# The operand of the gated mixer's short convolutions is kept in PSUM instead of SBUF

## The chip, the cores and the metric

The kernel runs on one core of a Trainium2 chip. The metric is the device time of one execution in microseconds; three runs of the kernel before and, later, of the kernel after are compared by their medians.

## The reference

Two model blocks run one after the other on 256 tokens of width 1024, all in float32. The first block has three kinds of attention, a gated MLP with a width-3 convolution and a per-layer embedding gate. The second has two layers, each a mixer, a cross attention to a memory and a squared-ReLU MLP. The mixer of its second layer (`c_mixer`) is a gated delta rule, and only the start of it matters here:

```python
def short_conv(x, w):
    K = w.shape[0]                               # 4 taps
    T = x.shape[1]                               # 256 tokens
    xp = jnp.pad(x, ((0, 0), (K - 1, 0), (0, 0)))
    return sum(xp[:, j:j + T] * w[j] for j in range(K))

qkv, gate, b, a = _split(h @ w_in, C_SIZES)      # 3072 channels of q, k, v
qkv = jax.nn.silu(short_conv(qkv, conv_w))       # per channel, along the tokens
q, k, v = _split(qkv, (GDN_QK, GDN_QK, GDN_VW))
q = l2norm(...); k = l2norm(...)                 # 8 heads of 128
```

`h` is the RMS-normed input. The kernel multiplies the un-normed operand by the weights and scales the product by the row factor `R` (one value per token) afterwards.

## The kernel before

Everything lies transposed: channels on the 128 partitions, the 256 tokens along the free axis. float32 products are made of three fp32r products: each operand is cut into a high and a low half, and hi*hi, hi*lo and lo*hi are summed in PSUM.

**Weights.** They come in 188 chunks through a ring of three. `fetch` (L438) loads a chunk in two halves of 128x1024. ScalarE (ACT) casts each half to `hi`, and then `lo` = raw - hi is made on VectorE (DVE) or on GpSimd (POOL); a hand-made list (`W["pool"]`) says how many of a chunk's two halves go to POOL.

**Products.** `gemm_ab` (L472) issues 48 matmuls of 128x256 into one PSUM tile, `pg`: a bank of 128x512 float32, that is 128 channels x 2 groups x 256 tokens. The pool of `pg` has two banks. So product n+2 goes into the bank of product n, and its first matmul waits until everything that reads product n there is done. Between its matmuls `pump` lets other work of the mixer issue its small matmuls at times that a planner's table gives; on TensorE (PE) the order is then fixed as written.

**Order on the other engines.** The framework orders the instructions of each engine by a timeline that it works out when the program is built, and adds every semaphore. An engine takes its instructions in that order. Two instructions on different engines that touch the same PSUM tile are kept in the order in which the program states them.

**The convolutions.** `conv` (L1441) runs twelve times. I number them: conv 1 to 4 are q and k of heads 0 to 3, conv 5 and 6 are values, conv 7 to 10 are q and k of heads 4 to 7, conv 11 and 12 are values. Each takes the product `ps`, scales it by `R` into an SBUF tile `u` (L1447, DVE, 128x512), and then, for each of its two groups, makes one output `cc[:, i]` of four taps: the first tap is a scaled copy on ACT, the other three are multiply-adds on DVE (`stt`, L377), each on `u` shifted by one, two or three tokens. `cc` lies in a part of the tile `Vm`, so in the trace a tap is `Vm<-u,cols` on ACT and `Vm<-u,cols,Vm` on DVE. `u` is one of four buffers that other temporaries share: the squares of q and k, the SiLU of v, three tiles of the gates and the output gates' SiLU.

**What follows a convolution.** For q and k (`qk_then`, L1464) ACT makes the SiLU (`K<-Vm`), then its squares (`u<-K`), and PE sums them with eight tiny matmuls (`ps<-one,u`). For v (`v_then`, L1481) ACT makes the SiLU (`u<-Vm`) and PE transposes it (`ps<-con,u`). When four heads are through, `group` (L1497) makes their norms and queues the decay matrices (`E<-acc,CC` on ACT, `X<-acc,E` on DVE, `acc<-K` and `acc<-Gh,sel` on PE), and `base` (L1545) solves 16x16 triangular blocks in a serial chain of small DVE steps (`t<-I,N` and `I<-t`).

**Gates and output gates.** `gates` (L1401) makes two rows of gate values per head with small DVE steps, two scans among them. After conv 12 come the products of the output gates (`gate`, L1656), which go through the same two banks.

Of the kernel before, what the change touches and what calls it, by code (L numbers as in the profile page):

```python
# [10 lines left out]
AF = mybir.ActivationFunctionType  # L11
ALU = mybir.AluOpType
# [3 lines left out]
T = 256  # L16
# [248 lines left out]
class Prog:  # L265
# [1110 lines left out]
    def c_mixer(self, x, R, rc, kv_head, K, Vm):  # L1376
        nc, tc = self.nc, self.tc
        with ExitStack() as es:
# [6 lines left out]
            ut = lambda shape=(128, 2, T): mx.tile(list(shape), F32, tag="u", name="u", bufs=4)  # L1385
# [48 lines left out]
            lastu = [None]  # L1434
# [6 lines left out]
            def conv(g, key, j0, j1, then):  # L1441
                ps = self.gemm_a(key, x)
                self.have_stats()
                self.until(lambda: cfree)
                n = cfree.pop(0)
                u = ut()
                lastu[0] = self.tt(u, ps, self.bc2(R), ALU.mult).ins.name  # L1447
                cc = csl[n]
                for i, j in enumerate((j0, j1)):
                    w = lambda t: self.col("cconv", 24 * t + j)  # L1450
                    self.act(cc[:, i], u[:, i], AF.Identity, scale=w(3))
                    for s in (1, 2, 3):
                        self.stt(cc[:, i, s:], u[:, i, 0:T - s], w(3 - s), cc[:, i, s:], ALU.mult, ALU.add)

                def gen():
                    while g and decays[0] < 4:
                        yield 0.3
                    yield from then(cc, n)

                self.spawn(gen())  # L1460
# [207 lines left out]
            def turn(j):  # L1668
# [12 lines left out]
                return gen  # L1681

            conv(0, ("cqk2", 0), 0, 8, qk_then(0))
            self.spawn(gates(), "g2")
            for g in range(2):
                for hd in range(4 * g, 4 * g + 4):
                    if hd:
                        conv(g, ("cqk2", hd), hd, 8 + hd, qk_then(hd))
                self.spawn(group(g))
                for i in (2 * g, 2 * g + 1):  # L1690
                    conv(0, ("cv", i), 16 + 2 * i, 17 + 2 * i, v_then(i))
# [85 lines left out]
```

## Time and profile before

| what | us |
|---|---|
| three runs | 1327.29, 1327.77, 1333.91 (median 1327.77) |
| the profiled execution | 1325.14 |
| its span, first to last instruction | 1323.4 |
| PE busy in the span | 1260.5 (95%) |
| DVE busy | 923.5 (70%) |
| ACT busy | 727.8 (55%) |
| POOL busy | 276.0 (21%) |

The span is what the trace covers; 1.7 us of the profiled execution lie around it. [...] A matmul's bar in the trace is longer than its share of the time, since matmuls are pipelined: the starts of two neighbours tell the pace. The convolutions stand between 805 and 925 us of the span. A row of the timeline gives the start, the length of one or of several merged instructions, the engine, the line, the output and inputs by the program's names, the shapes, the count, and in brackets how long the engine sat idle before it and what ended that.

### The profile page before, as it was taken

The numbers are of one execution on the slowest core, as the hardware profiler recorded it, in microseconds if no ns is written. First come the engines' busy times: TensorE is split into PE (matmuls) and PEld (weight loads), VectorE is DVE, ScalarE is ACT, GpSimd is POOL, SyncE is SP. The second block draws the span as 40 slices with busy tenths as digits, with TensorE's granted clock in tenths as the row PEclk, the third lists the DMA queues.
The fourth block names the chain that finished last, engine by engine and source line by source line (L and its number), as shares of the span: only waits on it lengthen the run. The fifth ranks groups of instructions, "written<-read, shape, count | busy, mean of one in ns | idle before, by whom it ended". The sixth has DMA issues, their size and how long they took to land. (4 is left out here: it accounts for less than half of the span.)

```text
span 1323.4 us, 24944 instructions
## 1 busy us (share of the span) xinstructions
PE 1260.5 (95%) x10195; PEld 1219.9 (92%) x10195; DVE 923.5 (70%) x1401; ACT 727.8 (55%) x1217; POOL 276.0 (21%) x160
## 2 busy tenths in 40 slices
PE   8899999999999999989999998888899989999997
PEld 8788889999999999989999998777799989999997
DVE  7877678777887665786666657999685375855564
ACT  6665475655586564655444447565543564644442
POOL 5500330000224200262000016434204370100000
PEclk8999989999999999999999999999999989999999
DMA  8433445555566544444655555333244343555551
GB/s 271 138 102 109 141 158 182 180 190 191 176 213 200 186 144 143 149 136 139 211 191 191 187 191 165 128 100 105 96 116 145 111 137 120 163 189 191 191 184 41
DMA packets 65698, 208.40 MB, mean 157 GB/s; under 512 B 13192, under 2 KB 14752, under 8 KB 65584
## 3 DMA queue, kind: packets, MB, share of 16 engines
q1 hardware_dynamic: 56976, 200.76, 46.5%
q0 software_dynamic: 1600, 4.88, 1.2%
q10 hardware_dynamic: 7008, 1.18, 0.5%
q8 instruction: 80, 1.31, 0.4%
q14 instruction: 34, 0.28, 0.1%
HBM read 205.32 MB, written 1.44 MB: 156 GB/s over the span
## 5 line engine op out<-in xcount | busy, mean ns | idle before, releaser
L357 ACT ACTIVATE hi<-raw 128x1024 fp32r<-128x1024 f32 (+1 forms) x378 | 378.7, 1047 | 218.5 <-PE pg L383 94.7
L374 DVE TENSOR_TENSOR lo<-raw,hi 128x1024 fp32r<-128x1024 f32 (+1 forms) x311 | 377.2, 1246 | 160.6 <-ACT hi L357 160.1
L383 PE MATMUL pg<-oh,hi 128*128 128x256 f32 x1632 | 467.9, 287 | 6.8 <-DVE u L374 2.8
L383 PE MATMUL pg<-ol,hi 128*128 128x256 f32 x1632 | 460.7, 282 | 5.2 <-DVE ol L377 4.5
L383 PE MATMUL pg<-oh,lo 128*128 128x256 f32 x1632 | 458.3, 281 | 0.0
L383 PEld LDWEIGHTS pg<-oh,hi 128*128 128x128 f32 x1632 | 309.4, 190 | 11.5 <-issue 5.4
L383 PEld LDWEIGHTS pg<-ol,hi 128*128 128x128 f32 x1632 | 309.1, 189 | 10.2 <-DVE ol L377 8.9
L383 PEld LDWEIGHTS pg<-oh,lo 128*128 128x128 f32 x1632 | 309.1, 189 | 0.0
L374 POOL TENSOR_TENSOR lo<-raw,hi 128x1024 fp32r<-128x1024 f32 (+1 forms) x67 | 169.9, 2550 | 627.3 <-ACT hi L357 610.4
L383 PE MATMUL acc<-mh,hi 128*128 128x256 f32 x688 | 192.2, 279 | 0.7 <-ACT mh L357 0.7
L383 PE MATMUL acc<-mh,lo 128*128 128x256 f32 x688 | 192.0, 279 | 0.0
L383 PE MATMUL acc<-mlo,hi 128*128 128x256 f32 x512 | 142.8, 279 | 0.0
L383 PEld LDWEIGHTS acc<-mh,lo 128*128 128x128 f32 x688 | 130.8, 190 | 0.0
L383 PEld LDWEIGHTS acc<-mh,hi 128*128 128x128 f32 x688 | 129.2, 188 | 1.1 <-ACT mh L357 0.9
L383 PE MATMUL pg<-hi,oh 128*128 128x256 f32 x352 | 105.1, 299 | 5.7 <-DVE u L374 3.5
L383 PE MATMUL pg<-lo,oh 128*128 128x256 f32 x352 | 101.4, 288 | 1.2 <-DVE lo L374 1.2
L383 PE MATMUL pg<-hi,ol 128*128 128x256 f32 x352 | 101.1, 287 | 0.0
L383 PEld LDWEIGHTS acc<-mlo,hi 128*128 128x128 f32 x512 | 96.2, 188 | 0.0
L383 PE MATMUL acc<-oh,hi 128*128 128x256 f32 x320 | 91.8, 287 | 0.5 <-ACT oh L357 0.5
L383 PE MATMUL acc<-ol,hi 128*128 128x256 f32 x320 | 90.5, 283 | 0.0
L383 PE MATMUL acc<-oh,lo 128*128 128x256 f32 x320 | 90.2, 282 | 0.0
L374 POOL TENSOR_TENSOR sq<-sq 128x512 f32<-128x512 f32 (+1 forms) x20 | 27.0, 1352 | 256.9 <-ACT sq L357 255.5
(382 smaller groups left out, 1924.9 us busy)
## 6 DMA issues: line engine op xcount, KB each, us to landing
raw<-in_w SPq DMA_DIRECT2D x374, 512.0 KB, 4.3
mt<-in_memT POOLq DMA_DIRECT2D x12, 256.0 KB, 3.7
h<-in_xT SPq DMA_DIRECT2D x4, 256.0 KB, 4.7
raw<-in_w SPq DMA_DIRECT2D x4, 256.0 KB, 5.0
fl<-in_rel SPq DMA_DIRECT2D x3, 256.0 KB, 4.3
gw<-in_gw POOLq DMA_DIRECT2D x2, 256.0 KB, 3.6
out<-h SPq DMA_DIRECT2D x2, 256.0 KB, 2.7
con<-in_con SPq DMA_DIRECT2D x1, 384.0 KB, 7.3
```

Of the source, the lines that this page charges most:

```text
L357: return self.nc.scalar.activation(out, in_, func, **k)
L374: return (eng or self.nc.vector).tensor_tensor(out, a, b, op)
L383: i = self.nc.tensor.matmul(out, lhsT=l, rhs=r, start=start, stop=stop, skip_group_check=True)
```

## The change

The scaled product is written back into the PSUM tile that it was read from, and all taps, on ACT and on DVE, read it there. The tile `u` of the convolution is gone. Nothing else in the program is edited; the number of instructions is the same, and so is what they compute.

```diff
-                u = ut()
-                lastu[0] = self.tt(u, ps, self.bc2(R), ALU.mult).ins.name
+
+                lastu[0] = self.tt(ps, ps, self.bc2(R), ALU.mult).ins.name
                 cc = csl[n]
                 for i, j in enumerate((j0, j1)):
                     w = lambda t: self.col("cconv", 24 * t + j)
-                    self.act(cc[:, i], u[:, i], AF.Identity, scale=w(3))
+                    self.act(cc[:, i], ps[:, i], AF.Identity, scale=w(3))
                     for s in (1, 2, 3):
-                        self.stt(cc[:, i, s:], u[:, i, 0:T - s], w(3 - s), cc[:, i, s:], ALU.mult, ALU.add)
+                        self.stt(cc[:, i, s:], ps[:, i, 0:T - s], w(3 - s), cc[:, i, s:], ALU.mult, ALU.add)
```

## Rows read from the trace of the kernel before

**Rows 1.** Stretch, length; busy us (count) of PE, PEld, DVE, ACT, POOL; PEclk; DMA.

```profile
805.00:925.00 120.00, 105.11 (x775) 97.31 (x773) 105.91 (x183) 68.25 (x120) 50.94 (x21) 0.96 0.41 127
...
840.00:844.00 4.00, 4.00 (x21) 4.00 (x22) 3.89 (x6) 2.66 (x4) 2.21 (x1) 0.57 0.17 62
...
881.40:919.10 37.70, 32.67 (x259) 31.88 (x258) 37.25 (x70) 16.49 (x28) 17.98 (x7) 0.95 0.48 147
```

**Rows 2.** Timeline of PE: waits in the stretch of the convolutions.

```profile
823.79 0.36 PE L383 MATMUL pg<-oh,hi 128*128 128x256 f32 x1
824.00 0.28 PE L383 MATMUL pg<-ol,hi 128*128 128x256 f32 x1
824.12 0.28 PE L383 MATMUL pg<-oh,lo 128*128 128x256 f32 x1
...
830.96 1.05 PE L383 MATMUL ps<-one,u 128*128 128x1 f32 x8 [1.98 <-ACT u L357]
...
839.96 0.36 PE L383 MATMUL pg<-oh,hi 128*128 128x256 f32 x1 [1.83 <-DVE u L374]
...
860.06 0.66 PE L395 MATMUL ps<-con,u 128*128 128x128 f32 x4 [0.90 <-ACT u L361]
862.87 1.47 PE L383 MATMUL acc<-K 128*128 128x256 f32 x4 [2.16 <-ACT E L361]
...
915.36 0.52 PE L383 MATMUL pg<-hi,oh 128*128 128x256 f32 x1 [2.21 <-DVE u L374]
```

**Rows 3.** Waits from 805 to 925 us: total, times, longest.

```profile
PE pg L383 <- DVE u L374: 6.3, 4, 2.2
```

**Rows 4.** DVE from 805 to 925 us by line and shape: count, busy, mean ns.

```profile
L377 DVE SCALAR_TENSOR_TENSOR Vm<-u,cols,Vm 128x253 f32<-128x253 f32 x24 | 23.4, 997 | 0.0
L377 DVE SCALAR_TENSOR_TENSOR Vm<-u,cols,Vm 128x254 f32<-128x254 f32 x24 | 14.9, 646 | 0.0
L377 DVE SCALAR_TENSOR_TENSOR Vm<-u,cols,Vm 128x255 f32<-128x255 f32 x24 | 14.4, 629 | 3.7 <-ACT Vm L357 3.6
...
L374 DVE TENSOR_TENSOR u<-pg,R 128x512 f32<-128x512 f32 x12 | 8.1, 678 | 0.4 <-PE pg L383 0.4
```

**Rows 5.** Instructions on the tile Vm: count, then ns shortest/median/longest.

```profile
L377 DVE SCALAR_TENSOR_TENSOR Vm<-u,cols,Vm x72: 350/476/2624, 814.0 to 918.7; 128x255 f32<-128x255 f32 x24, 128x254 f32<-128x254 f32 x24, 128x253 f32<-128x253 f32 x24
L357 ACT ACTIVATE Vm<-u,cols x24: 492/494/512, 813.5 to 915.8; 128x256 f32<-128x256 f32 x24
L357 ACT ACTIVATE Vm<-pg,memrc x16: 450/469/476, 411.1 to 1019.6; 128x256 f32<-128x256 f32 x16
```

**Rows 6.** Timeline of DVE: taps and a step of the block solve.

```profile
814.01 2.46 DVE L377 SCALAR_TENSOR_TENSOR Vm<-u,cols,Vm 128x255 f32<-128x255 f32 x6 [0.58 <-ACT Vm L357]
...
821.96 1.51 DVE L377 SCALAR_TENSOR_TENSOR Vm<-u,cols,Vm 128x255 f32<-128x255 f32 x1
...
826.18 3.40 DVE L377 SCALAR_TENSOR_TENSOR Vm<-u,cols,Vm 128x254 f32<-128x254 f32 x3
...
840.39 6.71 DVE L377 SCALAR_TENSOR_TENSOR Vm<-u,cols,Vm 128x255 f32<-128x255 f32 x6
...
881.40 5.03 DVE L377 SCALAR_TENSOR_TENSOR Vm<-u,cols,Vm 128x255 f32<-128x255 f32 x6 [1.00 <-ACT Vm L357]
...
903.16 2.21 DVE L374 TENSOR_TENSOR t<-I,N 64x121 f32<-64x121 f32 x1
...
908.66 5.00 DVE L377 SCALAR_TENSOR_TENSOR Vm<-u,cols,Vm 128x254 f32<-128x254 f32 x2
```

**Rows 7.** Timeline of POOL in the same stretch.

```profile
841.79 5.04 POOL L374 TENSOR_TENSOR lo<-raw,hi 128x1024 fp32r<-128x1024 f32 x2 [4.34 <-ACT hi L357]
```

**Rows 8.** DVE over the whole span by line and shape.

```profile
L377 DVE SCALAR_TENSOR_TENSOR q<-pg,R 128x512 f32<-128x512 f32 x8 | 5.5, 686 | 1.8 <-ACT R L361 1.7
...
L377 DVE SCALAR_TENSOR_TENSOR gg<-gg,hgh 128x512 f32<-128x512 f32 x2 | 1.3, 664 | 0.0
```

**Rows 9.** Timeline of ACT at the last product of the second MLP.

```profile
1299.33 0.38 ACT L357 ACTIVATE r<-pg 128x256 f32<-128x256 f32 x1 [1.54 <-DVE m L374]
```

## The prediction

> **What bounds the kernel now.** I read the busy shares first, and of the stretch from 805 to 925 us, where the convolutions stand. PE and DVE are each busy for some 105 of its 120 us, POOL for 51, and the granted clock is 0.96 [rows 1]. Over the whole span PE has 95%, so this is one of the places where PE is not full, and it is DVE that PE waits for. From 881.40 to 919.10 DVE is busy for 37.25 of 37.70 us [rows 1]; the chain of waits runs through it there.
>
> Next the waits of PE [rows 2]. Four products had to wait for the scaling of the product two before them, 6.3 us in all [rows 3]; the longest are 1.83 us at 839.96 and 2.21 us at 915.36. [...] Some 0.43 x 4 = 1.7 us is lost each time on top of the wait. Three waits are for what comes out of a convolution: 1.98 us at 830.96 (the squares of conv 2), 0.90 us at 860.06 (the SiLU of conv 6) and 2.16 us at 862.87 (the decays, whose norms stand behind that SiLU on ACT) [rows 2].
>
> Then the taps. Undisturbed, six of them take 2.46 us, 0.41 each [rows 6], and the median bar of one is 476 ns (neighbours overlap a little). But the means by shape are 997, 646 and 629 ns [rows 4, 5]: 24 x (997 + 646 + 629 - 3 x 476) = 20.3 us are lost. The bad ones take up to 2.6 us [rows 5], and they lie where POOL runs: the last of the six from 840.39 on are inside POOL's 841.79 to 846.83 [rows 6, 7]. A tap reads two SBUF tiles (`u` and `cc`), as does the step `t<-I,N` of 903.16, which is also stretched to 2.21 us [rows 6]. The scaling `u<-pg,R`, with one input in PSUM, has a mean of 678 ns over the same stretch, and `q<-pg,R` 686 [rows 4, 8]: in neither group is there room for one 2 us stall.
>
> **The change, part by part.**
>
> *Taps read PSUM.* Each tap keeps one SBUF input (`cc`), as the scaling has `R`. I take it that the 20.3 us go. The plain price stays: a multiply-add of 128x512 takes 686 ns with a PSUM input and 664 without [rows 8], so 0 to 22 ns for half the length; 72 x 0.02 = 1.4 us at most, taken as 0. ACT's copies gain 494 - 469 = 25 ns each [rows 5], 24 of them, 0.6 us, off the path.
>
> [...]
>
> *Scaling in place.* No row shows DVE writing PSUM. From below it is the scaling into SBUF, 678 ns [rows 4]; from above, if reading and writing the bank took turns, twice that, 12 x 0.68 = 8.1 us more. I take the lower, since a PSUM input alone costs next to nothing, and keep the upper for the range.
>
> *ACT and DVE take turns.* Both now read one bank. The trace has a case of this: at the last MLP product ACT's copy of the second half waited 1.54 us for DVE's read of the first half, with which it shares nothing but the bank [rows 9]. So the order becomes scaling, first tap, three taps, first tap of the other group, three taps. A turn to ACT and back costs DVE 0.58 us before its first tap [rows 6], 0.55 with the faster copy; before there was one turn per convolution, then there are two. That is 12 x 0.55 = 6.6 us of DVE time if nothing else fills it. ACT casts weights in that queue too, so the turn can be longer where a cast is in front.
>
> *The bank is held.* Before, product n+2 waits for the scaling of product n; then for its last tap. From the start of the scaling that is 0.68 + 0.55 + 1.23 + 0.55 + 1.23 = 4.2 us at best instead of 0.7, and product n+2 is queued on PE with all behind it.
>
> *Freed buffers.* The shared buffers lose their biggest user; the gates' tiles and the squares can only come earlier. Costed at nothing.
>
> **The sum,** by stretches. First, to 848 us. Product 4 starts at 823.79 without a wait [rows 2]. The taps of conv 2 end at 829.58 [rows 6]; without stalls they end 1.51 - 0.41 = 1.1 and 3.40 - 1.23 = 2.2 us sooner, and 0.55 later by the turn, at 826.8. So PE waits 3.0 us there, with a slow clock of 1.7 behind it; in return the 1.98 us at 830.96 vanish, being for the same taps. PE is 2.7 us late. Product 6 started at 839.96, just behind the scaling of conv 4. It now waits for that conv's taps: the scaling starts 0.8 us before 839.96, and is 3.3 us sooner with conv 2's stalls gone or not sooner at all (gate steps stand between); plus 4.2 us this is 840.1 to 843.4, while PE itself arrives at 839.96 - 1.83 + 2.7 = 840.8. I take 842.0: +2.0 us, with the slow clock there as before.
>
> Second, 848 to 877. Conv 4 loses 6.71 - 2.46 = 4.25 us of stalls [rows 6] and conv 5, alike, as much. The 0.90 and 2.16 us that PE waits for what follows them go: -3.1. Some slow clock behind them goes too, not counted.
>
> Third, 877 to 919, DVE's own stretch. Conv 8 loses 5.03 - 2.46 = 2.6 us, conv 11 loses 5.00 - 0.82 = 4.2, and one tap of conv 10 about 2.6 - 0.48 = 2.1 [rows 5, 6]. But here the steps `t<-I,N` stand between the taps and have two SBUF inputs: where a tap no longer stalls, the next such step does. So I take half of the last two, 3.1, and with 2.6 it is 5.7 us. Five more turns cost 2.8 us, half of them filled by those same steps: -4.3 on DVE. PE gets less of it, because products that started freely or behind a scaling now wait for taps. The last wait, at 915.36, is for the taps of conv 12, which come 4.3 us sooner but are 3.5 us later than the scaling: -0.8, and the slow clock behind it goes, -1.7. I take -2.5.
>
> +2.0 - 3.1 - 2.5 = -3.6 us. The profiled execution took 1325.14 us, so 1321.5; the median of the runs is 2.6 above it, so **1324.1 us**. What follows 919 us I let shift as a whole: 0.
>
> **The rivals.**
>
> *The stalls go and the holds cost nothing.* DVE is then early everywhere. Waits for products (6.3), the three behind convolutions (5.0) and two slow clocks (3.4) all vanish: -14.7, at 1313. For it: a hold of 4.2 us is shorter than a product, whose 48 matmuls at the pace of two neighbours, 824.00 and 824.12 [rows 2], take 5.8 us. Against it: conv 2 is late by its own chain.
>
> *The bank becomes the bound (slower).* Where DVE has other work between a product's end and its last tap, PE stands. Place: products 4, 6, 10, 11, 12 and the first output gate. If each waits 2.5 us and draws a slow clock of 1.7, that is 25 us; against it stand the 14.7 above: +10.5, at 1338. It decides from the point at which a hold exceeds the next product. For it: as the rows stand, with stalls, the taps of conv 4 take 6.7 us. Against it: without stalls none is over 5. [...]
>
> *It does nothing to the stalls' sum.* The stalls belong to POOL's runs, and the next instruction with two SBUF inputs inherits them, or the in-place write costs its upper bound: gain and loss cancel, 1328 with 2 us either way. For it: `t<-I,N` at 903.16. Against it: nothing of that kind stands between the taps before 862.
>
> **How the numbers follow.** My forecast has a chance of 0.42, all vanish 0.25, nothing 0.15, the bank 0.18. By bounds the forecast's own range is 1319 (no slow clock at products 4 and 6, and DVE's 4.3 us of the third stretch passed on in full) to 1328 (no turn filled, one more slow clock). For 8 in 10 the range goes into both outer cases, 1313.5 to 1336, leaving out about 0.08 below and 0.10 above. What a measurement can tell from no change is some 0.5%, 6.6 us: faster is below 1321.1, slower above 1334.4. Faster is the second case and a little of the first, 0.30; slower most of the bank's case, 0.17; the rest, 0.53, is the same.
>
> **What would show it.** Taps with a mean under 520 ns in all three shapes, none near 2.6 us; the scaling in place near 680 ns; ACT's second copy behind DVE's third tap; product 4 waiting for a tap; the waits at 830.96, 860.06 and 862.87 gone; `t<-I,N` and `lo` with more 2 us bars than before. Wrong it would be by product waits that add up to over 15 us, by taps that still stall, or by a scaling near 1.3 us.

## The result, and the profile after

Seven runs of each kernel, taken side by side: 1341.86 us for the kernel after (1334.45 to 1349.87) and 1331.17 us for the one before (1325.79 to 1333.91). The ratio is 1.0079, with a 95% interval of 1.0052 to 1.0106. The change makes the kernel slower, by 10.7 us between the medians. That is above the range that was predicted (1313.5 to 1336), and it is the rival "the bank becomes the bound".

The profiled execution of after took 1334.45 us, its span is 1332.7. PE issues the same matmuls in the same order in both kernels, so the start of one and the same matmul can be compared in the two traces. The trace of after already runs 5.7 us late at 804 us, where no instruction has been changed yet; executions differ by that much. What counts is what is added behind it:

| place (us of before) | after is late by | added in the stretch | predicted |
|---|---|---|---|
| 803.7, before the convolutions | 5.7 | | |
| 842.8, product 6 | 9.6 | +3.9 | +2.0 |
| 874.6, decays of heads 0 to 3 | 4.7 | -4.9 | -3.1 |
| 915.4, second output gate | 15.5 | +10.8 | -2.5 |
| 926.0, third output gate | 14.4 | -1.1 | 0 |
| end of the span | 9.3 | -5.1 | 0 |

In this pair the first two stretches come out as forecast, -1.0 in sum against -1.1, and the loss lies in the third. The last row is time given back behind the mixer; the variant with the change in conv 7 to 12 alone gives back 0.5 us there, so it is not counted on here. Up to 926 us the pair adds 8.7 us, to the end only 3.6. So the size of the loss is taken from the seven runs of each kernel, and the pair serves to show where it arises.

First the steps that held. DVE from 805 to 932 us by line and shape (count, busy, mean ns, idle before) in the kernel after:

```profile
L377 DVE SCALAR_TENSOR_TENSOR Vm<-pg,cols,Vm 128x255 f32<-128x255 f32 x24 | 11.4, 477 | 8.4 <-ACT Vm L357 8.0
L377 DVE SCALAR_TENSOR_TENSOR Vm<-pg,cols,Vm 128x253 f32<-128x253 f32 x24 | 11.3, 476 | 0.4
L377 DVE SCALAR_TENSOR_TENSOR Vm<-pg,cols,Vm 128x254 f32<-128x254 f32 x24 | 11.3, 475 | 0.4
L374 DVE TENSOR_TENSOR pg<-pg,R 128x512 f32<-128x512 f32 x12 | 8.3, 691 | 8.5 <-PE pg L383 8.4
L380 DVE TENSOR_SCALAR cV<-cV,rki 128x128 f32<-128x128 f32 x8 | 5.5, 736 | 0.0
...
L374 DVE TENSOR_TENSOR gC<-u 8x128 f32<-8x128 f32 x2 | 2.7, 1378 | 0.0
L374 DVE TENSOR_TENSOR t<-I,N 64x64 f32<-64x64 f32 x1 | 2.4, 2424 | 0.0
```

The three tap rows answer to those of [rows 4]: 477, 475 and 476 ns instead of 629, 646 and 997. The longest of the 72 lasts 483 ns, where POOL runs beside it or not. Scaling in place costs 691 instead of 678 ns. The stalls did not vanish altogether: the last three rows are small steps with SBUF inputs, and some of them last over 2 us (`cV` up to 2.40, `gC` 2.48, `t` 2.42).

Now what was lost. Waits of PE from 805 to 935 us (total, times, longest), after:

```profile
PE pg L383 <- DVE Vm L377: 12.4, 4, 4.9
...
PE pg L383 <- DVE I L1558: 4.4, 1, 4.4
...
PE pg L383 <- ACT hi L357: 1.1, 1, 1.1
```

These 17.9 us of waiting for a bank stand against the 6.3 of [rows 3], or 6.9 with one of 0.6 that is put down to a step `t`. The single waits, on PE's timeline:

```profile
824.22 0.35 PE L383 MATMUL pg<-oh,hi 128*128 128x256 f32 x1 [1.26 <-DVE Vm L377]
...
831.00 0.35 PE L383 MATMUL pg<-oh,hi 128*128 128x256 f32 x1 [1.10 <-ACT hi L357]
...
849.28 0.55 PE L383 MATMUL pg<-oh,hi 128*128 128x256 f32 x1 [4.95 <-DVE Vm L377]
...
894.04 0.55 PE L383 MATMUL pg<-oh,hi 128*128 128x256 f32 x1 [4.42 <-DVE I L1558]
...
911.30 0.55 PE L383 MATMUL pg<-oh,hi 128*128 128x256 f32 x1 [3.48 <-DVE Vm L377]
...
930.88 0.36 PE L383 MATMUL pg<-hi,oh 128*128 128x256 f32 x1 [2.67 <-DVE Vm L377]
```

These are products 3, 4, 6, 10 and 12 and the second output gate. Each of the first five starts just behind the last tap of the convolution that had its bank: conv 1 ends at 824.07, conv 2 at 830.86, conv 4 at 849.14, conv 8 at 893.89, conv 10 at 911.15. The names "hi" and "I" belong to instructions that ended beside that tap. At products 6, 10 and 12, behind waits of 3.5 to 5 us, the matmul's own bar is long (0.55 us), and the granted clock of TensorE over it is 0.50 of its full speed, the lower level (behind the wait at 839.96 of before it is 0.50 from 840.40 to 843.60); at products 3 and 4, behind 1.3 and 1.1 us, it is 1.00. Over the whole span it is 0.983 on average in before and 0.977 after. Stretch, length, busy us (count) of PE, PEld, DVE, ACT, POOL, granted clock, DMA:

```profile
805.00:925.00 120.00, 100.33 (x719) 94.14 (x718) 90.42 (x180) 65.77 (x116) 47.62 (x24) 0.91 0.39 122
...
849.00:853.00 4.00, 3.72 (x19) 3.75 (x20) 1.97 (x5) 2.14 (x4) 1.11 (x1) 0.57 0.75 236
...
881.40:919.10 37.70, 29.79 (x204) 28.81 (x204) 30.75 (x70) 17.59 (x28) 12.23 (x5) 0.84 0.38 119
```

Against [rows 1]: DVE is busy for 15.5 us less of the 120, and PE for 4.8 us less. But 120 us of after hold less work, since it is late. The same 787 matmuls, from the first row of the table above to the third output gate, first in before and then in after:

```profile
803.70:926.00 122.30, 106.41 (x787) 98.62 (x785) 108.21 (x188) 69.83 (x124) 51.17 (x22) 0.96 0.40 124
```

```profile
809.40:940.40 131.00, 110.14 (x787) 103.32 (x786) 94.59 (x189) 72.97 (x129) 46.98 (x21) 0.91 0.40 124
```

DVE, the engine that was to be relieved, was relieved by 13.6 us. PE stands for 20.9 us instead of 15.9: its waits for products rise from 7.9 (here with 1.1 of the third output gate) to 17.9, and its other waits fall by 5.0. The remaining 3.7 us are longer busy time at a lower clock, 0.91 instead of 0.96. Behind the wait at 849.28 the clock is at 0.57 on average from 849.00 to 853.00, and at 0.50 from 849.28 to 852.48.

Why the bank is held so long is seen in DVE's timeline of conv 4, from its scaling to its last tap, after:

```profile
838.72 0.70 DVE L374 TENSOR_TENSOR pg<-pg,R 128x512 f32<-128x512 f32 x1 [0.78 <-PE pg L383]
839.33 0.72 DVE L1419 TENSOR_TENSOR_SCAN u<-u,zero 8x128 f32<-8x128 f32 x2
...
840.75 1.21 DVE L374 TENSOR_TENSOR lo<-raw,hi 128x1024 fp32r<-128x1024 f32 x1
841.88 2.69 DVE L374 TENSOR_TENSOR gC<-u 8x128 f32<-8x128 f32 x2
844.50 0.47 DVE L377 SCALAR_TENSOR_TENSOR Vm<-pg,cols,Vm 128x255 f32<-128x255 f32 x1
844.89 0.54 DVE L374 TENSOR_TENSOR Gl<-u,Gh 8x384 fp32r<-8x384 f32 x1
845.36 0.98 DVE L377 SCALAR_TENSOR_TENSOR Vm<-pg,cols,Vm 128x254 f32<-128x254 f32 x2
846.25 0.69 DVE L374 TENSOR_TENSOR pg<-pg,R 128x512 f32<-128x512 f32 x1
846.88 2.65 DVE L377 SCALAR_TENSOR_TENSOR Vm<-pg,cols,Vm 128x255 f32<-128x255 f32 x6
```

Between the scaling at 838.72 and the first tap at 844.50 stand the gates' steps, a cast's low half and a step `gC` that lasts 2.5 us beside a run of POOL. (The six taps at 846.88 are three of conv 4 and three of conv 5.) POOL, after:

```profile
840.98 3.23 POOL L374 TENSOR_TENSOR lo<-raw,hi 128x1024 fp32r<-128x1024 f32 x1 [6.13 <-ACT hi L357]
845.44 4.67 POOL L374 TENSOR_TENSOR lo<-raw,hi 128x1024 fp32r<-128x1024 f32 x2 [1.22 <-ACT hi L357]
```

The same work on DVE in before:

```profile
835.11 2.93 DVE L1419 TENSOR_TENSOR_SCAN u<-u,zero 8x128 f32<-8x128 f32 x2
...
838.74 0.47 DVE L374 TENSOR_TENSOR gC<-u 8x128 f32<-8x128 f32 x2
839.14 0.67 DVE L374 TENSOR_TENSOR u<-pg,R 128x512 f32<-128x512 f32 x1
839.75 0.54 DVE L374 TENSOR_TENSOR Gl<-u,Gh 8x384 fp32r<-8x384 f32 x1
```

There most of it stood ahead of the scaling, which came 6.7 us behind the product's end (832.48 to 839.14), and the bank was free 0.7 us later. After, the scaling follows its product at once, and the same work stands inside the hold.

All twelve, from the bars of DVE (start of the scaling to the end of the last tap, and what DVE did in between): the mean hold is 7.83 us, of which 3.29 are the scaling and the six taps, 1.09 idle, waiting for ACT's first taps, and 3.45 other instructions of DVE's queue. The prediction had 4.2 us: 3.14 for the first item, 1.1 for the second, and nothing for the third.

Counted from the end of the product, where the bank could come free at the earliest, to its release (the end of the scaling before, of the last tap after):

| conv | 1 | 2 | 3 | 4 | 5 | 6 | 7 | 8 | 9 | 10 | 11 | 12 | mean |
|---|---|---|---|---|---|---|---|---|---|---|---|---|---|
| before, us | 6.5 | 0.7 | 8.2 | 7.3 | 9.6 | 8.4 | 4.1 | 1.7 | 6.1 | 8.2 | 9.9 | 10.3 | 6.75 |
| after, us | 10.5 | 7.9 | 8.0 | 10.5 | 7.4 | 5.9 | 13.5 | 9.9 | 8.9 | 9.9 | 10.8 | 8.9 | 9.35 |

The convolutions themselves are done sooner: the last tap comes 9.35 us behind the product on average, before it was 12.81. But the bank is free 2.6 us later.

### The profile page after: what moved, and what is told of

It is laid out like the page before. It is cut to its first block, busy times and chain, and to the rows that moved or that the text cites. A ratio compares the mean times of both kernels' runs of the same rounds, so it can differ in the third digit from the quotient of the medians.

```text
span 1332.7 us, 24944 instructions
## 1 busy us (share of the span) xinstructions
PE 1262.8 (95%) x10195; PEld 1221.8 (92%) x10195; DVE 907.9 (68%) x1401; ACT 727.6 (55%) x1217; POOL 271.7 (20%) x160
## 4 chain that ended last, share of the span: by engine, by line
PE 74%; DVE 15%; issue 3%; ACT 3%; DMA 3%; POOL 0%; DVEq 0%; SPq 0%; ACTq 0%; POOLq 0%
PE pg L383 42%; PE acc L383 28%; DVE ol L377 3%; PE ps L383 2%; DVE lo L374 2%; ACT hi L357 2%; DVE h L374 1%; DVE qq L374 1%; DVE t L374 1%; DVE Vm L377 1%; PE acc L395 1%; DMA raw<-in_w 1%; DVE cc L377 1%; DVE qk L377 1%; DMA ci<-di 1%
## 5 line engine op out<-in xcount | busy, mean ns | idle before, releaser
L383 PEld LDWEIGHTS pg<-ol,hi 128*128 128x128 f32 x1632 | 310.7, 190 | 10.7 <-DVE ol L377 9.0
L374 POOL TENSOR_TENSOR lo<-raw,hi 128x1024 fp32r<-128x1024 f32 (+1 forms) x67 | 166.0, 2491 | 640.9 <-ACT hi L357 633.8
```

What stands on the lines that cost most here:

```text
L374: return (eng or self.nc.vector).tensor_tensor(out, a, b, op)
L383: i = self.nc.tensor.matmul(out, lhsT=l, rhs=r, start=start, stop=stop, skip_group_check=True)
```

## The experiments

**The hold alone.** The taps read `u` in SBUF as in before, stalls and all. A copy of two columns of the product, which nobody needs, stands behind the last tap and keeps the bank until then.

```diff
-                        self.stt(cc[:, i, s:], u[:, i, 0:T - s], w(3 - s), cc[:, i, s:], ALU.mult, ALU.add)
+                        lastt = self.stt(cc[:, i, s:], u[:, i, 0:T - s], w(3 - s), cc[:, i, s:], ALU.mult, ALU.add)
+                hold = mx.tile([128, 2], F32, tag="hold", name="hold")
+                last = lastt.ins.name
+                self.order(self.nc.vector.tensor_copy(hold, ps[:, :, 0]), last)
```

> The convolution as before, with its scaled product in SBUF, but one tiny DVE copy reads the PSUM product behind the last tap, so that only the hold of the bank is added. If the hold is the cause: PE's waits for products rise from 6.3 us to over 15 us and the time is 8 us or more above before. If the turns between ACT and DVE on one bank are the cause: within 4 us of before, since there are no turns here. If the loss lies elsewhere: the same, within 4 us.

Measured: 1344.66 us, ratio 1.0082 (1.0061 to 1.0104). Its waits of PE, 805 to 935 us:

```profile
PE pg L383 <- DVE hold L1456: 12.8, 5, 7.0
```

The twelve copies take 146 ns each by the median, 1.8 us together. With 2.2 us that are put down to a step of the block solve it is 15.0 us, and one more wait, 6.0 us at 936.14, lies just outside that window. So a loss as large as that of the change comes from a hold alone, with no tap in PSUM, no scaling in place and no second turn. The hold is not quite the same one: the stalled taps stand in it, the last tap comes 9.96 us behind the product's end, and the copy ends at 10.04.

**One turn for each convolution.** The change, but both first taps on ACT come ahead, and DVE's six follow, the two groups alternating as in before.

```diff
+                u = ps
...
+                w = lambda t, j: self.col("cconv", 24 * t + j)
                 for i, j in enumerate((j0, j1)):
-                    w = lambda t: self.col("cconv", 24 * t + j)
-                    self.act(cc[:, i], ps[:, i], AF.Identity, scale=w(3))
-                    for s in (1, 2, 3):
-                        self.stt(cc[:, i, s:], ps[:, i, 0:T - s], w(3 - s), cc[:, i, s:], ALU.mult, ALU.add)
+                    self.act(cc[:, i], u[:, i], AF.Identity, scale=w(3, j))
+                for s in (1, 2, 3):
+                    for i, j in enumerate((j0, j1)):
+                        self.stt(cc[:, i, s:], u[:, i, 0:T - s], w(3 - s, j), cc[:, i, s:], ALU.mult, ALU.add)
```

> The product stays in its PSUM bank as in the change, but ACT makes both first taps before DVE makes its six, which alternate between the two groups: one turn and not two. If the turns are the cause: the extra time of the change goes, between 8 us below and 3 us above before. If the hold itself is the cause, one turn shortens it (from a mean of 8 us towards 5 us) but does not end it: 2 to 8 us above before, with waits for products still over 6 us.

Measured: 1337.52 us, ratio 1.0027 (1.0007 to 1.0047). The bank is released 9.05 us behind the product; the waits at products are 10.3 us in five for taps, and two of 4.2 and 2.1 us that are put down to a cast and to a step of the block solve. Better than the change, still slower than before. But the mean hold is 7.52 us and did not shrink towards 5, and in its trace the stretch from 804 to 926 us adds 8.4 us, nearly as in the change (8.7). What one turn saves is therefore not found in the trace and stays open.

**No turn at all.** The change, with the first taps on DVE instead of ACT.

```diff
-                    self.act(cc[:, i], ps[:, i], AF.Identity, scale=w(3))
+                    self.ts(cc[:, i], ps[:, i], w(3), ALU.mult)
```

> The change with the first taps on DVE too, so that only DVE reads the bank and no turn to ACT stands in a hold; DVE has 24 more instructions of some 0.4 us, 10 us in all, and ACT 12 us less. Theory, the turns between the two queues are what makes the holds 8 us and not 4.2: holds of 0.69 + 8 x 0.48 = 4.5 us where no other step stands between, product waits under half of the changed kernel's 14 us, and a ratio of 0.999 to 1.004, the DVE time put aside. Rival, it is the other work in DVE's own queue that makes them long: holds of 7 us and more, and a ratio of 1.006 to 1.012.

Measured: 1340.72 us, ratio 1.0073 (1.0044 to 1.0103). DVE's idle time in a hold falls from 1.09 to 0.38 us, but the hold is 8.09 us long: own work 4.06, other work 3.65. So it is not the turns that make the holds long, and the expectation's rival holds: DVE's other work is as large as in the change. Waits of PE from 805 to 935 us:

```profile
PE pg L383 <- DVE Vm L377: 13.9, 5, 5.5
PE pg L383 <- DVE I L1558: 6.1, 1, 6.1
```

**The change in one half of the convolutions.** `u` is `ps` for the convolutions named, an SBUF tile for the rest.

```diff
+            convs = [0]
...
-                u = ut()
+                convs[0] += 1
+                u = ps if convs[0] in (1, 2, 3, 4, 5, 6) else ut()
```

> The change in convolutions 1 to 6 only; 7 to 12 keep the scaled product in SBUF. Theory, the loss is the sum of single holds, each paid where a product stands behind it: the waits of the changed kernel in this part are 1.26 us at 824.22 and 4.95 us at 849.28, each with a slow clock of some 1.7 behind it, against the 1.83 and 2.9 us that the shorter taps give back: 3 to 8 us more than before, a ratio of 1.002 to 1.006, with those two waits for a tap and none from 880 us on. Rival of my prediction, the first stretches gain 1.1 us in sum (+2.0 and -3.1): a ratio of 0.999. Rival, the loss comes only from the stretch after 877 us, where DVE is full: 1.000 or under.

Measured: 1334.94 us, ratio 1.0023 (1.0002 to 1.0044), a small loss where the forecast for these convolutions was a gain of 1.1 us. PE waits for three taps, 7.1 us. With 7 to 12 in that list instead:

> The change in convolutions 7 to 12 only. Theory, single holds: the waits of the changed kernel here are 4.43 us at 894.04 and 3.48 us at 911.30 with a slow clock behind each, against the wait of 2.21 us that is gone: 4 to 7 us more than before, a ratio of 1.003 to 1.005, and together with the other half it makes up the 1.008 of the whole. Rival of my prediction: 2.5 us less, 0.998.

Measured: 1344.63 us, ratio 1.0100 (1.0071 to 1.0129). The last six carry the loss, and more of it than was expected from their two waits. The two halves add up to 1.0123, more than the 1.0079 of the whole, so they do not simply add. In the waits from 805 to 935 us of the last six:

```profile
PE pg L383 <- DVE I L1560: 6.2, 1, 6.2
PE pg L383 <- DVE Vm L377: 5.9, 2, 4.6
```

A third wait for a tap, 3.7 us at 939.83, lies behind that window. This is the stretch where DVE had no time to spare [rows 1], and where the casts, the decays and the block solve stand between the taps.

**Another bank.** The scaled product goes into a bank of the decays instead of SBUF (conv 7 stays in SBUF), so the taps read PSUM and the product's own bank is free behind the scaling. First with one turn, then with the change's own order of taps.

```diff
+            convs = [0]
...
-                u = ut()
+                convs[0] += 1
+                u = ut() if convs[0] == 7 else self.bank(1 + 2 * (convs[0] % 2)).rearrange("p (a t) -> p a t", a=2)
```

> As the kernel with one turn, but the scaled product goes into another PSUM bank, one of those of the attention-like lanes that are idle here (conv 7 alone keeps SBUF), so that the product's bank is free after the scaling. If the hold is the cause: 4 to 12 us below before, taps without stalls and waits for products under 6 us. If the turns alone are the cause: the same time as the kernel with one turn, within 3 us. If the loss lies elsewhere: about 10 us above before.

> The change's order of taps, two turns, with the scaled product in another PSUM bank. If the hold is the cause: at most the time of before, 0 to 8 us below it, and PE does not wait for a tap at the start of a product. If the turns are the cause: the time of the change, 8 us or more above before.

Measured: 1332.23 us, ratio 0.9996 (0.9976 to 1.0016), and 1333.34 us, 1.0001 (0.9983 to 1.0019). The loss is gone in both, so it was neither the PSUM operand nor the turns. But some 20 us of stalls on taps are gone as well (the longest of the 66 taps on that bank lasts 486 ns in the first and 484 in the second) and buy nothing; the gain of 4 to 12 us that was expected of the first did not come. Where that went, in the waits of the first of them from 805 to 935 us:

```profile
PE ps L383 <- ACT u L357: 8.7, 2, 6.8
PE acc L383 <- DVE I L1554: 4.6, 1, 4.6
```

No product waits for a tap any more. The 6.8 us are for the squares of conv 2: the program's order put the scaling of conv 3 (827.96) and steps of the gates ahead of conv 2's last taps (833.87), and one of these steps took 2.9 us beside POOL. On DVE:

```profile
827.96 0.69 DVE L374 TENSOR_TENSOR acc<-pg,R 128x512 f32<-128x512 f32 x1
...
831.04 2.90 DVE L374 TENSOR_TENSOR u<-u,R 8x512 f32<-8x512 f32 x1
833.87 1.24 DVE L377 SCALAR_TENSOR_TENSOR Vm<-acc,cols,Vm 128x253 f32<-128x253 f32 x3
```

The 4.6 us are for a decay whose bank conv 12 was using; in the kernel with two turns it is 4.9.

**Another bank, old order.** Only conv 3 to 6 and 8 to 10 go to the other bank, with one turn, and each scaling is kept behind the last tap of the convolution ahead.

```diff
+                u = self.bank(...) if convs[0] in (3, 4, 5, 6, 8, 9, 10) else ut()
+                sc = self.tt(u, ps, self.bc2(R), ALU.mult)
...
+                if lastt[0]:
+                    self.order(sc, lastt[0])
```

> The scaled products of convolutions 3 to 6 and 8 to 10 go to a bank of their own, the other five to SBUF as before; one turn for each convolution, taps in the order of before, and each scaling is kept behind the last tap of the convolution ahead of it, so that no later step passes conv 2's taps, and conv 11 and 12 keep off the banks of the decays. Theory, the tap stalls are worth something once nothing is held and no chain is made later by the order: the waits of 6.8 us for conv 2's squares and of 4.6 us for the decays that the two kernels with another bank had are gone, and the ratio is 0.994 to 0.998. Rival, the stalls cost PE nothing, or the next step with two SBUF inputs takes them over: 0.999 to 1.001, with the DVE time that the taps lose found again on other steps. My prediction's rival in which all waits vanish gives 0.989.

Measured: 1331.30 us, ratio 0.9981 (0.9954 to 1.0008). The interval leaves both theories standing. The trace says more: the bank is free 2.65 us behind the product on average, and from 804 to 915 us PE gains 11.0 us on before. Then the output gates take half of it away by 926. PE, and ACT in the same stretch:

```profile
924.83 0.58 PE L383 MATMUL pg<-hi,oh 128*128 128x256 f32 x1 [8.28 <-ACT u L361]
```

```profile
911.12 0.47 ACTq L1723 DMA_DIRECT2D di<-I  x1
913.46 0.45 ACTq L1723 DMA_DIRECT2D di<-N  x1
...
916.21 1.79 ACTq L1724 DMA_DIRECT2D ci<-di  x2
918.10 0.63 ACT L361 ACTIVATE u<-Vm 128x512 f32<-128x512 f32 x1 [3.96 <-DMA di<-N]
...
923.94 0.84 ACT L361 ACTIVATE u<-pg,rc 128x256 f32<-128x256 f32 x2
```

The third output gate needs the bank of the first, whose SiLU (923.94) stands on ACT behind transfers that wait for transfers, and behind the norms that follow them.

**The transfers on another queue.** The kernel above, with the transfers of `blocks_in`, four for each half of the heads, issued by POOL; and, as a control, that edit on the kernel before.

```diff
-        self.nc.scalar.dma_start(d, I)
-        self.nc.scalar.dma_start(ci, d.rearrange("(k b) r c -> (b r) k c", k=8))
+        self.nc.gpsimd.dma_start(d, I)
+        self.nc.gpsimd.dma_start(ci, d.rearrange("(k b) r c -> (b r) k c", k=8))
```

> The kernel with another bank and kept order, and the four small transfers that bring a solved block back to 128 partitions are issued from POOL's queue instead of ACT's. In the former kernel PE had gained 12.2 us between 804 and 917 us and then waited 8.3 us at 924.83 for the SiLU of the first output gate, which stood on ACT behind transfers that wait for transfers (911.12 to 918.00). Theory, that wait is ACT's queue: it falls to under 3 us, PE keeps 5 to 10 of the 12 us, ratio 0.991 to 0.996. Rival, something else is late next there (the decays of heads 4 to 7, the squares, a lo half on POOL behind a waiting transfer): 0.997 to 1.000.

> The kernel before with only those four transfers moved to POOL's queue. In before no PE wait stands behind them, so the move by itself should be worth nothing: 0.998 to 1.002. Below 0.997 the gain of the other kernel would not be the bank's.

Measured: 1327.60 us, ratio 0.9974 (0.9943 to 1.0006), and 1328.42 us for the control, 0.9980 (0.9949 to 1.0011). The wait falls from 8.3 to 5.2 us, not to under 3, and from 804 to 915 us PE gains 7.4 us in this execution. What ends the wait now is still that SiLU. With the transfers gone from its queue, ACT still stands ahead of it, now for the last tap of conv 12:

```profile
921.38 0.63 ACT L361 ACTIVATE u<-Vm 128x512 f32<-128x512 f32 x1 [5.96 <-DVE Vm L377]
```

So the transfers were not the whole of that wait, as the expectation's rival had it. Neither run is told apart from no change, nor from each other, so it stays open whether the bank is worth anything here.

**Other work behind the last tap.** The change, and what DVE is given later in the program's order may not pass a convolution's last tap.

```diff
+    def late(self, i, eng=None):
+        if self.held and not eng:
+            self.order(i, self.held)
+        return i
...
+                self.held = lastt.ins.name if key != ("cv", 3) else None
```

`late` is wrapped around each DVE instruction that `tt`, `stt` and `ts` issue.

> The change as it is, and what DVE is given after a convolution in the program's order is kept behind that convolution's last tap, so that less of DVE's other work stands inside a hold. In the changed kernel the twelve holds have a mean of 7.83 us, from the bars of DVE: 3.29 the scaling and the six taps, 1.09 waiting for ACT's first taps, 3.45 other work of DVE (casts, gate steps, steps of the decays and of the block solve). In the new order most of it is out of holds 1 to 9; from conv 10 on the block solve stays in. Theory, it is that other work which my sum left out: holds 1 to 9 under 6 us, holds 10 to 12 as before, the waits for a tap at products 3, 4, 6 and 10 gone or under 1 us, ratio 1.000 to 1.004. Rival, the hold costs whatever its length, or the work that is put off is missed elsewhere as much: 1.006 to 1.010.

Measured: 1342.97 us, ratio 1.0094 (1.0060 to 1.0129): the time of the rival. The holds of conv 1 to 9 did shrink, from 7.84 to 6.14 us on average, and their other work by two thirds. But what was put off now stood ahead of the next scaling: product 3, for one, ends at 830.54, and its scaling starts at 836.29. From the product's end to the release it is 9.01 us for conv 1 to 9, nearly the 9.18 of the change. So the length of the hold, which the prediction and this expectation both looked at, is only a part: what PE sees is the time from the product's end to the last reader's end, and DVE's queue fills that either way. The run's time itself does not decide between the two theories. The waits behind conv 1 to 9 fell from 11.7 to 8.8 us, while a wait of the decays for a step that was put off rose from 2.3 to 5.3. And conv 12, which was to stay as it was, is held for 13.58 us instead of 4.80; the second output gate waits 7.84 us for it, at 938.88.

**Short holds only.** The change in conv 1, 5 and 6.

```diff
-                u = ut()
+                convs[0] += 1
+                u = ps if convs[0] in (1, 5, 6) else ut()
```

> The change in convolutions 1, 5 and 6 only, the three of the changed kernel whose holds (5.50, 5.52 and 5.91 us) are not longer than a product (5.8 us). Theory, a hold costs nothing up to the length of the next product: no wait of PE for a tap over 0.5 us, and what the shorter taps of conv 5 and 6 give back is kept (my sum had 3.1 us there): ratio 0.997 to 1.000. Rival, each hold costs by itself: 1.002 (three twelfths of the loss) or more.

Measured: 1329.32 us, ratio 0.9979 (0.9951 to 1.0007). The three holds do not cost by themselves. In the new order conv 5 was held for 7.76 us, though, and PE waited for taps for 2.3 us in two waits, so the bound of 0.5 us failed, and the interval cannot tell a gain from nothing.

## Why the prediction was wrong

**Tap stalls go: right.** 20.3 us were named; the bars of the 72 taps add up to 34.3 us instead of 54.5, so 20.2 are gone.

**PSUM operand costs nothing: right.** 475 to 477 ns with PSUM against a median of 476 with SBUF [rows 5].

**Scaling in place near 0.68: right.** 0.69.

**Two turns, 1.1 us for a convolution: right on average.** 1.09, but that it fits so well is luck: the single convolutions lie between 0.16 us, where other work fills the turn, and 3.22. That ACT and DVE take turns at the bank came true too: at 928.71 ACT's second copy of conv 12 waits 1.58 us for DVE's third tap, and DVE's next tap 0.54 us for that copy. What was missed is small: the three taps of a group are neighbours now and each waits for the one ahead, 0.51 us a tap (three in 1.52 us at 836.42) instead of 0.41. It is the order and not PSUM: in the run with another bank and one turn, four alternating taps on PSUM take 1.63 us at 835.30, 0.41 each, as the six in 2.46 of before [rows 6].

**A slow clock of 1.7 us behind a long wait: right in size, not at product 4.** The 0.43 is 1 - 0.57, from the 4.00 us at 840.00 in [rows 1]; from 915.30 to 919.30 the clock of before is 0.57 too. After, it is 0.57 from 849.00, 0.62 from 894.00 and 0.50 from 911.30 over 4 us each, but 1.00 from 831.00, behind product 4's wait of 1.10.

**The first two stretches: right in sum in the one pair of traces**, +3.9 and -4.9 for +2.0 and -3.1. Product 6 does wait for conv 4's taps, and the waits at 830.96, 860.06 and 862.87 of [rows 2] are gone. The parts fit less well. Product 4 was to wait 3.0 us; it waits 1.10, and product 3, which was not named, 1.26. Product 4's start was also misread: the row at 823.79 is its fourth matmul, and it starts at 822.64, so the same working would have given 4.2 us. And the runs with the change in the first six convolutions alone lose (1.0023), where the forecast of -1.1 us would be 0.999, so the agreement of the sum is in part luck.

**The hold of 4.2 us "at best": the step that failed.** It was the sum of what the convolution itself does, and it was used as what the bank sees. The measured hold is 7.83 us, of which 3.45 us are other instructions of DVE's own queue, with the stalls some of them met beside POOL; from the product's end to the release it is 9.35 us instead of 6.75. For the third stretch this gave -2.5 us where +10.8 came: there the prediction gave PE a part of DVE's gain and took off 3.5 us once, at conv 12, where every bank from conv 7 to 11 was free later than before, by 0.9 to 9.4 us. The rows needed for it were at hand: DVE was busy for 37.25 of 37.70 us [rows 1], so anything that spans several of its instructions had to take in its other work.

**The rival "the bank becomes the bound"** gave +10.5 us and a chance of 0.18, and the argument against it, "without stalls none is over 5", is the failed step again. Eleven of twelve holds are over 5 us. It had the mechanism right; that its number comes so close is in part luck. It set waits of 25 us with the clock against 14.7 that vanish. In the pair of traces, product waits add 10.0 us and the clock 3.7, other waits take off 5.0, and products 4, 6, 10 and 12 wait as it named, but 11 and the first output gate do not, and 3 and the second gate do. That the change loses, at 1.0079, is not for a reason of rate: 0.9996 with the operand in a PSUM bank that no product waits for shows that it is the held bank and not the speed of an operation.

**The stalls' sum.** That other steps inherit them was the third rival. It happens in part: `gC` 3.1 instead of 0.9 us and `cV` 5.9 instead of 4.2 between the first and the last tap; with the other bank and two turns `t<-I,N` 12.8 instead of 8.1. Most of the gain, 13.6 us of busy time, reached DVE and stopped there.

## What to carry to other kernels

To keep an operand in the buffer that a product is written to turns each of its readers into a reason for the next product to wait: here the waits for products rose from 7.9 to 17.9 us. Price that from the end of the product to the end of the last reader, with everything the reading engine has in its queue, above all where it is busy all the time (here 37.25 of 37.70 us), and not as the sum of the readers' own times. Price it product by product: the mean alone does not give the time, since the run with one turn had 9.05 us and lost 3.6 us by its ratio, the change 9.35 and 10.5. An engine's stalls are worth removing only as far as the chain behind them, here three different ones (a bank, the squares of a norm, the SiLU of a gate), lets the time through: 13.6 us less of busy DVE came with 10.7 us more in the time.

## What the runs show of the hardware

- A multiply-add with one input in PSUM was not stretched beside POOL: at most 483 ns in 72, the six at 846.88 beside POOL's 4.67 us from 845.44 among them, while the same operation with two SBUF inputs reached 2624 [rows 5], and in the kernel after a step of 8x128 with SBUF inputs took 2.5 us.
- Reading and writing the same PSUM bank in one DVE instruction took 13 ns more than reading it and writing SBUF: 691 against 678 ns for 128x512.
- Three multiply-adds in a row, each on the result of the one ahead, followed each other at 0.51 us (three in 1.52 at 836.42 of after); two chains alternating did at 0.41 us, on SBUF (six in 2.46 [rows 6]) as on PSUM (four in 1.63, with another bank and one turn).
- A transfer that waits on ACT's queue held up the copy behind it: in the kernel after, ACT's second copy of conv 8 waits 1.94 us for the transfer that the one ahead of it needs:

```profile
886.49 0.41 ACTq L1710 DMA_DIRECT2D dn<-cpt  x1
...
888.71 0.52 ACTq L1711 DMA_DIRECT2D N<-dn  x1
889.28 0.47 ACT L357 ACTIVATE Vm<-pg,cols 128x256 f32<-128x256 f32 x1 [1.94 <-DMA dn<-cpt]
```
